# New cost figures for the block inverse in an emission planner, and smaller buffer demands in one scan

## The chip, the cores and the metric

The kernel runs on one core of a Trainium2 chip. The metric is the device time of one execution in microseconds. The profile is one execution, taken by the hardware profiler. Its engines are TensorE (PE for matmuls, PEld for weight loads), VectorE (DVE), ScalarE (ACT), GpSimd (POOL) and SyncE (SP), which issues all the DMAs.

## The reference, cut to what matters

Two layers run over 512 tokens of a main stream (x, width 1024) and 256 tokens of a context stream (c). In each layer one input projection feeds three head groups: a short gated convolution, a gated DeltaNet in both directions (4 heads of 128), and a spatial-gating MLP. An output projection and a SwiGLU feed-forward layer follow. In the last layer the context gives only the two final DeltaNet states.

```python
m = eye + where(strict, kkt * dmat * bc[..., None], 0)      # one triangular system per chunk, head and direction
sol = triangular_solve(m, rhs, lower=True, unit_diagonal=True)
u, w = sol[..., :dv], sol[..., dv:]
def _delta_update(s, w_c, u_c, kt_c, gl_c):
    v_new = u_c - w_c @ s
    return v_new, s * exp(gl_c) + kt_c.T @ v_new
```

The kernel solves these systems by inverting them, with chunks of 128 tokens, and then scans over the chunks with the state.

## The kernel before, in words

**A planner writes the program.** Each piece of the model is a Python generator (a task). While the program is built, a planner keeps one planned clock for each engine (`clk`: t for TensorE, v for VectorE, a for ScalarE, p for GpSimd, s and d for SyncE and the DMAs). Each helper (`vtt`, `vtrans`, `act`, `matmul`, `dma`) emits one instruction and calls `spend`, which adds a written cost, in us, to its engine's clock, after the operands' planned times. A task yields either a planned time, from which it may go on, or a condition. `run_tasks` always resumes the task with the lowest priority number of those that can go on at TensorE's planned time. The order in which the helpers are called is the order of the instructions on each engine, for SP's DMAs too. The costs are in no instruction: they only decide the order, which of two engines a copy goes to (`lighter`), and which buffer is taken.

**Buffers.** There are 66 small slots (128 x 512) and 13 large ones (128 x 1024). `room=n` in `gtile` lets a task go on only while n small slots are free. `stash` spills a finished tile to DRAM when its planned time comes, and `unstash` reads it back.

**Weights.** A `Feed` loads a weight tile (`wf`), rounds it to a high part (`wh`, on ACT or DVE) and subtracts to get a low part (`wl`, on DVE). The dense products read both parts.

**The block inverse** runs four times, once for each stream and layer: context of layer 0 (here c0), main of layer 0 (x0), context of layer 1 (c1), main of layer 1 (x1). `block_inverse` gathers the 32 x 32 diagonal blocks of eight matrices (four heads, two directions) into one tile, `iva`: for four of them by copies, for four by small transposes on DVE. One large transpose follows, then 31 row steps of two DVE instructions each (`ivt` = product, `ivv` = difference), each step followed by `yield self.pace()`, which waits until TensorE's planned clock is within 2 us of DVE's. Two large transposes write `iva` and `ivb`. Then four tasks (`substitute`) build `td` and `U` for two matrices each: GpSimd clears the tile, eight block copies fill `td` and `U` (64 for an inverse), matmuls form the product Q and join the blocks, and U is the inverse. `gdn_scan` waits for U. For context of layer 1 it runs with `kv_only`: it updates the states and gives no output.

```python
def vtt(self, out, a, b, op):
    self.nc.vector.tensor_tensor(out=out, in0=a, in1=b, op=op)
    self.spend("v", 0.07 + 1.04 * self.size(out), [out], [a, b])   # size: thousands of elements per partition
```

Tile names in the trace are those with which a slot was first named, so that a tile of one role may stand under another name.

Of the kernel before, what the change touches and what calls it, by code (L numbers as in the profile page):

```python
# [8 lines left out]
AF = mybir.ActivationFunctionType  # L9
ALU = mybir.AluOpType  # L10
AX = mybir.AxisListType

P = 128
# [269 lines left out]
class Builder:  # L283
# [221 lines left out]
        self.nc.vector.scalar_tensor_tensor(out=out, in0=in0, scalar=scalar, in1=in1, op0=op0, op1=op1)  # L505
        self.spend("v", 0.13 + 1.04 * self.size(out), [out], [in0, in1])

    def vtt(self, out, a, b, op):
        self.nc.vector.tensor_tensor(out=out, in0=a, in1=b, op=op)  # L509
        self.spend("v", 0.07 + 1.04 * self.size(out), [out], [a, b])  # L510

    def vts(self, out, a, s1, s2, op0, **kw):
        self.nc.vector.tensor_scalar(out, a, s1, s2, op0=op0, **kw)
# [9 lines left out]

    def vtrans(self, out, in_):
        self.nc.vector.transpose(out, in_)  # L525
        self.spend("v", 0.07 + 1.04 * self.size(out), [out], [in_])

    def ptt(self, out, a, b, op):
        self.nc.gpsimd.tensor_tensor(out=out, in0=a, in1=b, op=op)
# [2 lines left out]
    def round(self, out, in_):  # L532

        n = self.size(out)
        (self.act if self.lighter(v=0.07 + 0.52 * n, a=0.09 + 0.83 * n) == "a" else self.vcopy)(out, in_)

    def copy(self, out, in_):

        n = self.size(out)
        if in_.space == bass.MemoryType.PSUM:  # L540
            e = self.lighter(v=0.07 + 1.04 * n, a=0.05 + 0.83 * n)
        else:
            e = self.lighter(v=0.07 + 0.52 * n, a=0.09 + 0.83 * n)
        {"v": self.vcopy, "a": self.act}[e](out, in_)
# [784 lines left out]
    def block_inverse(self, st, G):  # L1329

        n, T = st.n, st.T
        yield lambda: "inverse" not in self.ev
        self.ev.add("inverse")
        self.wanted = 4
        yield lambda: self.lroom() >= 0
        self.wanted = 0
        bufs = [self.blk(s, 1024) for s in ("iva", "ivb", "ivv", "ivt")]
        C, X, V = (b.ap.rearrange("p (a b) -> p a b", b=32) for b in bufs[:3])
        tmp = bufs[3].ap
        if 8 * n < 32:  # L1340
            self.pset(C[:, 8 * n:, :], 0.0)
        for j in (0, 4, 1, 5, 2, 6, 3, 7):
            lt3 = G["Lt"][j].ap.rearrange("p (t c) -> p t c", c=P)
            for q in range(4):
                r = slice(32 * q, 32 * q + 32)
                blkd = lt3[r, :, r]
                dst = C[r, n * j:n * j + n, :]
                if j < 4:
                    self.copy(dst, blkd)
                else:  # L1350
                    self.vtrans(dst, blkd)
                self.pset(blkd, 0.0)
            yield self.pace()
        self.vtrans(X, C.rearrange("p s f -> p f s"))
        vf = bufs[2].ap
        self.pset(vf, 0.0)
        self.pset(vf[:, 0:1024:33], 1.0)
        for j in range(31):
            a, b = j + 1, 31 - j
            tm = tmp[:, :a * b].rearrange("p (i k) -> p i k", k=b)  # L1360
            xj = X[:, a:, j:j + 1].rearrange("p k o -> p o k")
            self.vtt(tm, V[:, 0:a, j:j + 1].to_broadcast([P, a, b]), xj.to_broadcast([P, a, b]), ALU.mult)
            self.vtt(V[:, 0:a, a:], V[:, 0:a, a:], tm, ALU.subtract)
            yield self.pace()

        E1, E2 = C, X
        self.vtrans(E1.rearrange("p s i -> p i s"), V)
        self.vtrans(E2.rearrange("p s k -> p k s"), V.rearrange("p i k -> p k i"))
        bufs[2].free()
        bufs[3].free()  # L1370
        sl = lambda t: slice(P * t, P * t + P)

        def substitute(js):
            yield self.room(4)
            td = self.blk("td", T)
            self.pset(td.ap, 0.0)
            v3 = lambda ap: ap.rearrange("p (t c) -> p t c", c=P)
            for j in js:
                lt, fwd = G["Lt"][j], j < 4
                us, ts = (E2, E1) if fwd else (E1, E2)  # L1380
                yield self.room(3)
                U = self.blk("U", T)
                self.pset(U.ap, 0.0)
                for q in range(4):
                    r = slice(32 * q, 32 * q + 32)
                    self.copy(v3(td.ap)[r, :, r], ts[r, n * j:n * j + n, :])
                    self.copy(v3(U.ap)[r, :, r], us[r, n * j:n * j + n, :])
                pq = yield from self.gtile(td.ap, lt.ap, room=2)
                for t in range(n):
                    self.matmul(pq[:, sl(t)], lt.ap[:, sl(t)], td.ap[:, sl(t)])  # L1390
                lt.free()
                Q = self.blk("Q", T)
                self.act(Q.ap, pq[:, :T], AF.Copy, scale=-1.0)

                for rows, cols in ((((0, 96), (32, 128)), ((0, 64), (64, 128)), ((0, 32), (96, 128))) if fwd else
                                   (((0, 128), (0, 96)), ((64, 128), (0, 64)), ((64, 128), (0, 32)))):
                    r, c = slice(*rows), slice(*cols)
                    pv = yield from self.gtile(Q.ap, U.ap)
                    for t in range(n):
                        self.matmul(v3(pv)[r, t, c], v3(Q.ap)[:, t, r], v3(U.ap)[:, t, c])  # L1400
                    if c.stop - c.start == 96:
                        self.vtt(v3(U.ap)[r, :, c], v3(pv)[r, :n, c], v3(U.ap)[r, :, c], ALU.add)
                    else:
                        r = slice(96, 128) if cols == (0, 32) else r
                        self.copy(v3(U.ap)[r, :, c], v3(pv)[r, :n, c])
                Q.free()
                G["U"][j] = U
            td.free()

        for i in range(self.NSUB):  # L1410
            self.spawn(K["psub"], substitute(range(i, 8, self.NSUB)))
        yield lambda: len(G["U"]) == 8
        bufs[0].free()
        bufs[1].free()
        self.ev.discard("inverse")
        G["inverse"] = True
# [25 lines left out]
    def gdn_scan(self, st, G, states, kv_only, keep_last):  # L1442

        n = st.n
# [4 lines left out]
        v3 = lambda ap: ap.rearrange("p (h c) -> p h c", c=P)  # L1449
# [3 lines left out]
        def direction(d):  # L1453
            for i in range(n):
# [2 lines left out]
                col = lambda key, h: G[key][:, t, 4 * d + h:4 * d + h + 1]  # L1457
                s, last = states[d], i == n - 1 and not keep_last
                if s is not None:
                    ps = yield from self.gtile(s, room=5)  # L1460
                    for h in hs:
                        self.matmul(ps[:, cs[h]], G["kT"][h].ap[:, c], s[:, cs[h]])
                    r = self.blk("r")
                    for h in hs:
                        self.stt(r.ap[:, cs[h]], ps[:, cs[h]], col("ego", h), vn[h].ap[:, c], ALU.mult, ALU.add)
                pv = yield from self.gtile(*([r.ap] if s is not None else []), room=4)
                for h in hs:
                    b = r.ap[:, cs[h]] if s is not None else vn[h].ap[:, c]
                    self.matmul(pv[:, cs[h]], G["U"][4 * d + h].ap[:, c], b)
# [48 lines left out]
        for d in K["dirs"]:  # L1518
            self.spawn(0, direction(d))
# [647 lines left out]
```

## Time and profile before

| | us |
|---|---|
| median of 3 runs | 1806.54 (1805.84 to 1809.01) |
| the profiled execution: its time | 1808.4 |
| the profiled execution: its span, first to last instruction | 1806.7 |
| PE busy / PEld busy | 1736.9 / 1488.1 |
| DVE busy / ACT busy / POOL busy | 1319.5 / 777.8 / 103.6 |
| mean granted TensorE clock | 0.985 of full speed |

The 1.7 us between time and span lie before the first and after the last instruction. Busy times are sums over the span, and the engines overlap: what an idle gap costs is read from the stretch in which it lies.

### The profile page before, as it was taken

The numbers are of one execution on the slowest core, as the hardware profiler recorded it, in microseconds if no ns is written. First come the engines' busy times: TensorE is split into PE (matmuls) and PEld (weight loads), VectorE is DVE, ScalarE is ACT, GpSimd is POOL, SyncE is SP. The second block draws the span as 40 slices with busy tenths as digits, with TensorE's granted clock in tenths as the row PEclk, the third lists the DMA queues.
The fourth block names the chain that finished last, engine by engine and source line by source line (L and its number), as shares of the span: only waits on it lengthen the run. The fifth ranks groups of instructions, "written<-read, shape, count | busy, mean of one in ns | idle before, by whom it ended". The sixth has DMA issues, their size and how long they took to land.

```text
span 1806.7 us, 27473 instructions
## 1 busy us (share of the span) xinstructions
PE 1736.9 (96%) x10271; PEld 1488.1 (82%) x10271; DVE 1319.5 (73%) x2510; ACT 777.8 (43%) x1685; POOL 103.6 (6%) x268
## 2 busy tenths in 40 slices
PE   6999999979999999999999999999899999999998
PEld 2588888869799888888788898888789798888886
DVE  1689869957769977633688866679968897667746
ACT  3764446253564232111364346467443754322222
POOL 0001002000000000000002000002000000000000
PEclk8899999989999999999999999999999999999999
DMA  8742212235578755533352435532334683234234
GB/s 285 251 141 84 83 40 71 85 105 171 158 222 269 227 183 187 161 111 113 96 167 84 126 107 167 164 92 79 107 96 136 197 231 101 90 109 128 82 94 139
DMA packets 288869, 250.14 MB, mean 138 GB/s; under 512 B 14544, under 2 KB 219350, under 8 KB 288736
## 3 DMA queue, kind: packets, MB, share of 16 engines
q1 hardware_dynamic: 288736, 248.40, 45.2%
q8 instruction: 80, 1.31, 0.3%
q14 instruction: 53, 0.43, 0.1%
HBM read 233.28 MB, written 15.07 MB: 137 GB/s over the span
## 4 chain that ended last, share of the span: by engine, by line
PE 34%; DVE 9%; ACT 3%; DMA 3%; issue 1%; POOL 1%; DVEq 0%; SPq 0%; POOLq 0%; ACTq 0%
PE ps L496 33%; DVE wl_l L509 2%; DMA wf_l<-in_w_in_dram 1%; DVE ivt_l L509 1%; DMA wf_l<-in_w_ffn_in_dram 1%; DVE ivv_l L509 1%; ACT wh_l L553 1%; DVE x_b L505 1%; DVE dt_b L509 1%; DVE acc_b L509 1%; PE ps L501 1%; DVE iva_l L525 0%; DVE ivb_l L525 0%; ACT xn_b L553 0%; ACT junk L553 0%
## 5 line engine op out<-in xcount | busy, mean ns | idle before, releaser
L496 PE MATMUL ps<-hh_b,wh_l 128*128 128x256 f32 (+2 forms) x2640 | 724.0, 324 | 7.6 <-DVE hh_b L505 3.3
L496 PE MATMUL ps<-hh_b,wl_l 128*128 128x512 f32 (+1 forms) x1960 | 655.2, 334 | 1.9 <-DVE wl_l L509 1.9
L496 PEld LDWEIGHTS ps<-hh_b,wh_l 128*128 128x128 f32 (+1 forms) x2640 | 458.5, 190 | 53.7 <-DVE hh_b L505 4.6
L496 PE MATMUL ps<-hl_b,wh_l 128*128 128x512 f32 (+3 forms) x1360 | 484.7, 357 | 0.0
L509 DVE TENSOR_TENSOR wl_l<-wf_l,wh_l 128x1024 fp32r<-128x1024 f32 (+1 forms) x310 | 375.7, 1214 | 145.2 <-ACT wh_l L553 115.8
L496 PEld LDWEIGHTS ps<-hh_b,wl_l 128*128 128x128 f32 x1960 | 374.1, 191 | 40.6 <-DVE wl_l L509 2.8
L553 ACT ACTIVATE wh_l<-wf_l 128x1024 fp32r<-128x1024 f32 (+2 forms) x218 | 226.9, 1043 | 324.7 <-PE ps L496 117.5
L496 PEld LDWEIGHTS ps<-hl_b,wh_l 128*128 128x128 f32 (+1 forms) x1360 | 257.7, 190 | 37.3 <-issue 1.7
L496 PE MATMUL ps<-wh_l,ah_b 128*128 128x512 f32 x576 | 201.6, 390 | 0.0
L496 PE MATMUL ps<-wl_l,ah_b 128*128 128x512 f32 x424 | 165.3, 390 | 1.1 <-DVE wl_l L509 1.1
L505 DVE SCALAR_TENSOR_TENSOR macc_b<-mw_b,csilu,macc_b 128x512 f32<-128x512 f32 x182 | 132.6, 747 | 16.2 <-DMA mw_b<-in_w_mod_dram 9.7
L496 PEld LDWEIGHTS ps<-wh_l,ah_b 128*128 128x128 f32 x576 | 108.1, 188 | 22.5 <-issue 0.3
L517 DVE CAST wh_l<-wf_l 128x1024 fp32r<-128x1024 f32 (+1 forms) x95 | 64.9, 684 | 69.2 <-PE ps L496 46.1
L496 PE MATMUL ps<-wh_l,al_b 128*128 128x512 f32 x272 | 105.9, 389 | 0.0
L496 PEld LDWEIGHTS ps<-wl_l,ah_b 128*128 128x128 f32 x424 | 79.6, 188 | 18.0 <-DVE wl_l L509 1.9
L553 ACT ACTIVATE ah_b<-at_b 128x512 fp32r<-128x512 f32 (+1 forms) x76 | 40.6, 538 | 121.4 <-DVE at_b L509 121.4
L553 ACT ACTIVATE at_b<-ps 128x512 f32<-128x512 f32 (+1 forms) x70 | 33.6, 481 | 119.6 <-PE ps L496 114.4
L496 PE MATMUL ps<-wh_l,yh_b 128*128 128x512 f32 x192 | 73.8, 402 | 0.1
L509 DVE TENSOR_TENSOR at_b<-ps,at_b 128x512 f32<-128x512 f32 (+1 forms) x70 | 38.4, 549 | 43.7 <-PE ps L496 43.7
L496 PE MATMUL ps<-wl_l,yh_b 128*128 128x512 f32 x160 | 62.8, 393 | 0.0
L509 DVE TENSOR_TENSOR ivt_l<-ivv_l,ivb_l 128x31 f32<-128x31 f32 (+15 forms) x124 | 60.0, 484 | 3.4
L509 DVE TENSOR_TENSOR acc_b<-ps,acc_b 128x512 f32<-128x512 f32 x92 | 59.6, 683 | 3.0 <-PE ps L496 3.0
(528 smaller groups left out, 2183.8 us busy)
## 6 DMA issues: line engine op xcount, KB each, us to landing
wf_l<-in_w_ffn_in_dram SPq DMA_DIRECT2D x132, 512.0 KB
mw_b<-in_w_mod_dram SPq DMA_DIRECT2D x208, 256.0 KB
wf_l<-in_w_ffn_out_dram SPq DMA_DIRECT2D x66, 512.0 KB
wf_l<-in_w_in_dram SPq DMA_DIRECT2D x64, 512.0 KB
wf_l<-in_w_o_dram SPq DMA_DIRECT2D x32, 512.0 KB
us_b<-sd SPq DMA_DIRECT2D x26, 256.0 KB
xd<-x_b SPq DMA_DIRECT2D x20, 256.0 KB
x_b<-xd SPq DMA_DIRECT2D x20, 256.0 KB
```

The lines of the kernel that those rows point to most:

```text
L496: self.nc.tensor.matmul(out, lhsT, rhs, start=start, stop=stop, skip_group_check=more)
L501: self.nc.tensor.transpose(out, in_, self.ident[:m, :m])
L505: self.nc.vector.scalar_tensor_tensor(out=out, in0=in0, scalar=scalar, in1=in1, op0=op0, op1=op1)
L509: self.nc.vector.tensor_tensor(out=out, in0=a, in1=b, op=op)
L517: self.nc.vector.tensor_copy(out, in_)
L553: self.nc.scalar.activation(out=out, in_=in_, func=func, **kw)
```

## The change

The costs of the block inverse's own DVE and ACT instructions are replaced in the planner, and a state-only scan asks for 3 and 2 free small slots where it asked for 5 and 4. No instruction's operands are changed.

```diff
-    def vtt(self, out, a, b, op):
+    def vtt(self, out, a, b, op, fixed=0.07, each=1.04):
         self.nc.vector.tensor_tensor(out=out, in0=a, in1=b, op=op)
-        self.spend("v", 0.07 + 1.04 * self.size(out), [out], [a, b])
+        self.spend("v", fixed + each * self.size(out), [out], [a, b])
...
     def vtrans(self, out, in_):
         self.nc.vector.transpose(out, in_)
-        self.spend("v", 0.07 + 1.04 * self.size(out), [out], [in_])
+        self.spend("v", 0.13 + 1.85 * self.size(out), [out], [in_])
...
+    def copy_block(self, out, in_):
+
+        n = self.size(out)
+        if self.lighter(v=0.16 + 0.55 * n, a=0.21 + 0.85 * n) == "a":
+            self.nc.scalar.activation(out=out, in_=in_, func=AF.Copy)
+            self.spend("a", 0.21 + 0.85 * n, [out], [in_])
+        else:
+            self.nc.vector.tensor_copy(out, in_)
+            self.spend("v", 0.16 + 0.55 * n, [out], [in_])
...
                 if j < 4:
-                    self.copy(dst, blkd)
+                    self.copy_block(dst, blkd)
                 else:
                     self.vtrans(dst, blkd)
...
-            self.vtt(tm, V[:, 0:a, j:j + 1].to_broadcast([P, a, b]), xj.to_broadcast([P, a, b]), ALU.mult)
-            self.vtt(V[:, 0:a, a:], V[:, 0:a, a:], tm, ALU.subtract)
+            self.vtt(tm, V[:, 0:a, j:j + 1].to_broadcast([P, a, b]), xj.to_broadcast([P, a, b]), ALU.mult, 0.17, 1.92)
+            self.vtt(V[:, 0:a, a:], V[:, 0:a, a:], tm, ALU.subtract, 0.2)
...
-                    self.copy(v3(td.ap)[r, :, r], ts[r, n * j:n * j + n, :])
-                    self.copy(v3(U.ap)[r, :, r], us[r, n * j:n * j + n, :])
+                    self.copy_block(v3(td.ap)[r, :, r], ts[r, n * j:n * j + n, :])
+                    self.copy_block(v3(U.ap)[r, :, r], us[r, n * j:n * j + n, :])
...
-                    ps = yield from self.gtile(s, room=5)
+                    ps = yield from self.gtile(s, room=3 if kv_only else 5)
...
-                pv = yield from self.gtile(*([r.ap] if s is not None else []), room=4)
+                pv = yield from self.gtile(*([r.ap] if s is not None else []), room=2 if kv_only else 4)
```

The copy that `copy_block` replaces was planned at 0.07 + 0.52 n on DVE and 0.09 + 0.83 n on ACT.

## Rows read from the trace of the kernel before

**Rows 1.** The page's busy time: us, share of the span, instructions.

```profile
PE 1736.9 (96%) x10271; PEld 1488.1 (82%) x10271; DVE 1319.5 (73%) x2510; ACT 777.8 (43%) x1685; POOL 103.6 (6%) x268
```

**Rows 2.** Windows of 20 us: PE, PEld, DVE, ACT, POOL busy, PEclk, DMA share, GB/s.

```profile
180.00:200.00 20.00, 17.28 (x86) 13.72 (x85) 19.35 (x40) 6.57 (x10) 2.17 (x8) 0.91 0.28 79
...
360.00:380.00 20.00, 8.69 (x65) 8.31 (x64) 13.62 (x41) 13.12 (x35) 3.67 (x7) 0.74 0.38 122
...
440.00:460.00 20.00, 16.62 (x93) 13.89 (x92) 14.90 (x31) 11.86 (x41) 5.00 (x5) 1.00 0.73 240
...
1020.00:1040.00 20.00, 16.84 (x112) 15.89 (x111) 15.16 (x27) 12.75 (x31) 0.32 (x1) 0.83 0.68 185
...
1300.00:1320.00 20.00, 14.26 (x74) 11.34 (x73) 18.05 (x46) 10.07 (x27) 1.57 (x2) 0.83 0.10 27
...
1740.00:1760.00 20.00, 20.00 (x90) 16.57 (x89) 8.35 (x10) 3.98 (x5) 0.00 (x0) 1.00 0.32 105
```

**Rows 3.** One window of 4 us behind the gap of x0.

```profile
376.00:380.00 4.00, 4.00 (x26) 3.89 (x27) 2.86 (x11) 2.24 (x7) 0.00 (x0) 0.53 0.00 0
```

**Rows 4.** Groups and tiles, block inverse: busy and mean ns, or ns min/median/max.

```profile
L509 DVE TENSOR_TENSOR ivt_l<-ivv_l,ivb_l 128x31 f32<-128x31 f32 (+15 forms) x124 | 60.0, 484 | 3.4
L509 DVE TENSOR_TENSOR ivv_l<-ivv_l,ivt_l 128x31 f32<-128x31 f32 (+15 forms) x124 | 42.4, 342 | 3.7
L525 DVE STREAM_TRANSPOSE ivb_l<-iva_l 128x1024 f32<-128x1024 f32 x4 | 8.4, 2092 | 0.4
L525 DVE STREAM_TRANSPOSE iva_l<-lt_b 32x128 f32<-32x128 f32 x32 | 9.6, 301 | 0.8
L517 DVE COPY U_b<-iva_l 32x128 f32<-32x128 f32 x18 | 3.9, 219 | 0.2
L553 ACT ACTIVATE td_b<-iva_l x30: 252/305/313, 209.7 to 1306.9; 32x128 f32<-32x128 f32 x18, 32x64 f32<-32x64 f32 x12
```

**Rows 5.** ACT's timeline where x0, c1 and x1 end: start, us, idle before.

```profile
357.93 0.63 ACT L553 ACTIVATE td_b<-iva_l 32x128 f32<-32x128 f32 x2 [10.14 <-issue]
358.58 0.39 ACT L553 ACTIVATE z_b<-ps 128x256 f32<-128x256 f32 x1
...
1021.56 2.12 ACT L553 ACTIVATE U_b<-iva_l 32x64 f32<-32x64 f32 x8 [13.01 <-DVE iva_l L525]
1023.71 1.06 ACT L553 ACTIVATE wh_l<-wf_l 128x1024 fp32r<-128x1024 f32 x1
...
1299.24 0.96 ACT L553 ACTIVATE td_b<-iva_l 32x128 f32<-32x128 f32 x3 [10.04 <-DVE iva_l L525]
...
1300.59 1.15 ACT L553 ACTIVATE vt_b<-ps 128x256 f32<-128x256 f32 x4
```

**Rows 6.** PE's timeline at the four inverses.

```profile
194.47 0.44 PE L501 MATMUL ps<-ident,vn_b 128*128 128x128 f32 x2 [2.72 <-ACT vn_b L553]
...
360.89 2.02 PE L496 MATMUL ps<-td_b,lt_b 128*128 128x128 f32 x16
...
375.83 6.26 PE L496 MATMUL ps<-U_b,Q_b 128*96 128x96 f32 x64 [11.31 <-ACT Q_b L553]
...
1024.82 0.58 PE L496 MATMUL ps<-hh_b,wh_l 128*128 128x256 f32 x1 [2.00 <-ACT wh_l L553]
...
1308.15 1.12 PE L496 MATMUL ps<-wst,vt_b 128*64 128x128 f32 x8 [4.97 <-ACT ac_b L553]
```

**Rows 7.** SP and ACT in the timeline of x0's gap.

```profile
365.36 0.39 SPq L472 DMA_DIRECT2D wf_l<-in_w_o_dram  x1
...
369.48 1.06 ACT L553 ACTIVATE wh_l<-wf_l 128x1024 fp32r<-128x1024 f32 x1 [4.31 <-DMA wf_l<-in_w_o_dram]
```

**Rows 8.** DVE and POOL in the same stretch.

```profile
363.36 2.31 DVE L517 COPY U_b<-ivb_l 32x128 f32<-32x128 f32 x2
...
363.88 1.45 POOL L547 MEMSET U_b<- 128x512 f32 x3
```

**Rows 9.** DVE's timeline at the state-only scan's first product.

```profile
1065.55 0.69 DVE L509 TENSOR_TENSOR v_b<-ps,bt_c 128x512 f32<-128x512 f32 x1 [0.81 <-PE ps L496]
```

## The prediction, made before the changed kernel was run

> **What bounds the kernel now.** I read the page's busy times first [rows 1]. PE is busy for 1736.9 of 1806.7 us, so only 69.8 us of the span are open to an edit that changes nothing but order, plus what a slow clock costs. The Trainium skill speaks against this reading (Perfetto Trace Analysis, Identifying the Most-Contended Engine): matmul busy time does not tell how near TensorE is to its limit, and the share of weight loads is to be used. By that rule up to 1806.7 - 1488.1 = 318.6 us would be open. The trace does not bear that out here: in a stretch late in the feed-forward layer where PE has no gap and a full clock, PEld is busy for 16.57 of 20 us, 83% [rows 2]. The page's 82% is thus what back-to-back products look like in this kernel, and I keep the 69.8.
>
> Next I looked for the gaps, with windows of 20 us. Each of the four inverses has one near its end [rows 2]: 20 less PE's busy time is 2.72 at c0, 11.31 at x0, 3.16 at c1 and 5.74 at x1, together 22.9 us. Behind each the granted clock is lower for a while (half speed is the lower of its two levels, 1.2 GHz). One less the clock, times 20, bounds the cost: 1.8 at c0, 3.4 at c1, 3.4 at x1. At x0 most of the slow time lies in the gap itself, so I take the stretch after it, 4 busy us at 0.53: 0.47 x 4 = 1.9 [rows 3]. That makes 10.5. What the change can give back at the inverses is therefore at most 22.9 + 10.5 = 33.4 us, 1.8%.
>
> Then I asked the timelines what holds PE in each gap. **In ACT's queue the block copies stand too early.** Before the first copy out of the transposed tile ACT sits idle for 10.14 us at x0, 13.01 at c1 and 10.04 at x1, and the instruction right behind is something that PE or DVE wants [rows 5]: at x0 a gate tile (z_b), at c1 the rounding of a weight (wh_l), at x1 the token-major copy (vt_b). PE then waits 2.00 for that wh_l at c1, and 4.97 at x1 for the normalised vt [rows 6]; there the row names another tile of ACT, but what the product reads is vt. At x0 the chain is longer: late z_b copies hold back spills on SP, the next output-projection weight is issued only at 365.36, ACT waits 4.31 for it with its rounding, and Q's copy stands behind that [rows 7], so that PE loses 11.31 [rows 6]. At c0 PE waits 2.72 for an ACT step on a value tile [rows 6]; I put that down to DVE's queue before it, which is busy for 19.35 of 20 us there [rows 2].
>
> So the planner thought the inverse done about 10 to 13 us before it was.
>
> **The change part by part.** Per inverse, the written costs before and after, and what the rows say [rows 4]:
> - Row steps: the products and differences cover the sum of (j+1)(31-j), 5456 elements. Before: 62 x 0.07 + 2.08 x 5.456 = 15.7 us. After: 31 x 0.37 + 2.96 x 5.456 = 27.6. Measured: (60.0 + 42.4) / 4 = 25.6. The planner gains 11.9.
> - Three large transposes: 1.13 before and 2.02 after, measured 2.09: 2.7 more.
> - Sixteen small transposes, 32 x 128: 0.20 before, 0.37 after, measured 0.30: 2.6 more.
> - Eighty block copies of that size: DVE 0.14 to 0.23, measured 0.22; ACT 0.20 to 0.32, measured 0.305. About 0.11 each, 8.6 over two engines. The ratio of the two engines' costs hardly moves (0.70 to 0.72), so the split between them should stay.
>
> The first three make 17.2 us on DVE before the copies can start, against a measured ACT wait of 10 to 13. The new costs thus cover the lag that I see, and overshoot it somewhat.
>
> Nothing of this is executed: no instruction becomes faster or goes away. What moves: row steps are spread over more of TensorE's planned time, since each waits until DVE's planned clock is within 2 us; other DVE work (wl, value tiles, normalisation) goes between them; block copies go behind roundings and gate copies in ACT's queue; and with them the spills and loads in SP's queue and the clears of td and U in POOL's. Cost of the moved instructions themselves: nothing, since their DVE and ACT time is the same; DVE's load in these windows (19.35 of 20 at c0 [rows 2]) is the cover that is thin, and without it a late wl costs PE its full lateness.
>
> What I count as given back, between nothing and 33.4:
> - c1: all of 3.2 + 3.4 = 6.6. A wh_l simply stands behind a copy that should come later.
> - x1: two thirds of 5.7 + 3.4, 6.1. The copies of vt can go first, but normalisation still shares DVE with the last transposes.
> - x0: half of 11.3 + 1.9, 6.6. The first part of its chain is ACT's early wait, the second is a weight that arrives late.
> - c0: half of 2.7 + 1.8, 2.3, as the order on DVE is only partly mended.
>
> Sum 21.6. Against it: work that goes ahead of the row steps makes the inverse end later, and behind each x inverse the scan has then less dense work beside it. At x0 PE begins with td at 360.89, only 3 us after the first copy, so nothing is spare there [rows 5, 6]. Some 80 us later PE already has a gap of 20 - 16.62 = 3.4 [rows 2]; I take that once more for each of x0 and x1, and 2.7, the smallest gap above, for a new order elsewhere: 9.5. The bounds of this term are 0 and 17.2 a place.
>
> **The looser room in the state-only scan: nothing.** Its first product's DVE step at 1065.55 waited 0.81 for PE, not for a buffer [rows 9], and the states it gives are read only by the scan behind x1, whose copies start at 1299.24 [rows 5], over 230 us later. Without that cover it could cost or give a microsecond. It may matter as a permission where the new order leaves fewer free slots.
>
> **A price the planner still leaves out.** Two block copies on DVE took 2.31 us instead of 0.44 while POOL cleared tiles [rows 8, 4]. The Trainium skill (SBUF — State Buffer, Who interferes with whom) says that such a DVE copy and a GpSimd instruction exclude each other for their whole length. By the row this costs 1.9 us in one place, and DVE idles afterwards. As a mechanism of this kernel: twelve clears an inverse, 1.45 / 3 = 0.48 us each on x, could hold a copy each time: 5.8 at each x inverse and half that at each c inverse, 17 in all.
>
> **Sum.** 1808.4 - 21.6 + 9.5 = 1796.3 for a profiled execution. The profiled one stands 1.9 above the median of the runs shown, so the median should be 1794.5.
>
> **The rivals.** About 0.2%, 3.6 us, is what a measurement of this kernel can tell from no change: faster means under 1802.9, slower over 1810.1.
> - *Part of the stalls go, some come back* (my forecast): 1794.5, own range 1784 to 1802.5. Chance 0.54.
> - *All of it comes back and nothing is lost*: 1806.5 - 33.4 = 1773, or down to 1784 with a loss. For it: the same sign at x0, c1 and x1 [rows 5]. Against: at x0 the late weight [rows 7]. Chance 0.11.
> - *The stall only moves*: ACT no longer stands before the copies, but PE waits instead for Q and U, as the inverse's chain on DVE is no shorter, and DVE is full. 1803 to 1810. The change then does nothing for the time. Chance 0.12.
> - *Slower: at x0 the dense work runs out.* If the copies leave up to 17.2 us later and no gate or projection product is left for PE, its gap grows from 11.3 by as much. The other places give 15.0 - 9.5 = 5.5; so this decides once x0's gap grows by over 9.1 us, to more than 20.4. At its full price: 1806.5 - 5.5 + 17.2 = 1818. For it: no slack at x0. Against: DVE's work is the same, and the lag of 10 us already happens. Chance 0.20.
> - *Slower by the port rule*: more copies fall beside clears, 17 us on DVE, of which PE would have to see over 16. 1811. Only one pair of copies shows it. Chance 0.03.
>
> **How the numbers follow.** Faster: 0.54 + 0.11 = 0.65. Same: 0.12. Slower: 0.20 + 0.03 = 0.23. The predicted time is the first case's. The range runs from 1779, which leaves out half of the second case, to 1814, which leaves out about half of the fourth: some 0.15 in all.
>
> **What would show it.** In the changed profile the ACT waits before the first copy out of iva should fall from 10 to 13 us to under 4, the row steps should be further apart with wl between them, and the clock behind each inverse should stay near 1. Instruction counts and mean durations should be the same to within a few copies that changed engine. Wrong would be: ACT waits as long as before (the planner's lag had another cause), the gap at x0 over 20 us, or a new gap of several us between 440 and 480 or after x1's scan. If the inverse windows mend and the total does not, the loss stands outside them, in the order of the feed-forward layers.

## The result, and the profile after

| | before | after |
|---|---|---|
| median of 6 runs, us | 1807.22 (1805.55 to 1810.94) | 1826.01 (1825.20 to 1831.35) |
| ratio after / before | | 1.0095, 95% interval 1.008 to 1.011 |
| the profiled execution / its span | 1808.4 / 1806.7 | 1825.2 / 1823.5 |
| mean granted TensorE clock | 0.985 | 0.983 |

The kernel became 0.95% slower, some 17 us by the ratio. The prediction was 1794.5 us with a range up to 1814.

The first view is the page's busy time (as [rows 1]).

```profile
PE 1743.0 (96%) x10271; PEld 1489.0 (82%) x10271; DVE 1315.0 (72%) x2490; ACT 784.0 (43%) x1711; POOL 100.2 (5%) x268
```

The counts of PE and POOL are the same; DVE has 20 instructions fewer and ACT 26 more, so more than a few copies chose the other engine. The span is 16.8 us longer: PE is idle for 80.5 us instead of 69.8, and busy for 6.1 us more with the same number of instructions. The Trainium skill (Perfetto Trace Analysis, Identifying the Most-Contended Engine) says that TensorE's headroom is to be judged by MFU (the matmul rate over the peak) and by the busy time of its weight loads, and not by that of its matmuls. The trace agrees in so far that PEld grew by 0.9 us only, so the 6.1 us are the same work taking longer and not more work.

Next, windows of 20 us (as [rows 2]; columns PE, PEld, DVE, ACT, POOL busy, PEclk, DMA share, GB/s).

```profile
360.00:380.00 20.00, 15.62 (x70) 12.03 (x69) 19.04 (x46) 8.07 (x14) 0.00 (x0) 0.83 0.54 179
380.00:400.00 20.00, 15.47 (x67) 11.67 (x66) 16.79 (x20) 10.51 (x22) 2.13 (x4) 0.99 0.80 240
400.00:420.00 20.00, 12.49 (x77) 11.66 (x78) 16.41 (x37) 16.41 (x39) 6.04 (x10) 0.66 0.43 141
420.00:440.00 20.00, 17.76 (x182) 17.14 (x180) 12.48 (x25) 16.36 (x38) 1.05 (x2) 1.00 0.58 163
440.00:460.00 20.00, 18.76 (x154) 17.79 (x155) 10.19 (x16) 5.85 (x14) 0.00 (x0) 0.83 0.38 116
...
1040.00:1060.00 20.00, 17.19 (x139) 16.87 (x140) 14.46 (x26) 12.78 (x26) 0.00 (x0) 1.00 0.69 189
...
1180.00:1200.00 20.00, 16.29 (x114) 15.65 (x115) 12.12 (x23) 13.75 (x30) 0.70 (x1) 0.83 0.39 111
...
1320.00:1340.00 20.00, 17.85 (x100) 14.15 (x99) 16.14 (x39) 8.35 (x18) 2.10 (x3) 1.00 0.46 124
```

The one gap of 11.31 at x0 is gone; five windows in a row with smaller gaps stand in its place, three of them with a slow clock. I add up, over all windows of a stretch, PE's idle time and (1 - PEclk) x 20. The second term also counts a slow clock while PE is idle, which costs nothing, so it is a bound:

| stretch, us | before | after |
|---|---|---|
| 180 to 360 | 2.8 + 1.8 = 4.6 | 2.6 + 1.8 = 4.4 |
| 360 to 540 | 16.5 + 5.2 = 21.7 | 22.4 + 13.8 = 36.2 |
| 540 to 980 | 2.4 + 0.0 = 2.4 | 4.9 + 0.0 = 4.9 |
| 980 to 1240 | 9.7 + 5.2 = 14.9 | 12.6 + 3.4 = 16.0 |
| 1240 to 1480 | 10.7 + 3.4 = 14.1 | 10.7 + 0.0 = 10.7 |

So x0 and what follows it lose 14.5 us by these sums, more of it (8.6) in clock than in idle time (5.9). The layer-1 inverses together are a little better.

What PE waits for (us in all, times, the longest): the wait for the normalised stream (tile xn_b) has doubled from 12.8 us, and ACT's Q, the 11.3 of [rows 6], is gone.

```profile
PE ps L501 <- ACT xn_b L563: 24.1, 9, 8.6
PE ps L496 <- DMA mw_b<-in_w_mod_dram: 6.7, 3, 4.6
PE ps L496 <- DVE wl_l L509: 5.7, 8, 1.6
```

The timelines around x0's end, DVE, POOL, ACT and PE (start, us, idle before). The first line is of the kernel before, the others are of the changed one:

```profile
357.70 2.15 DVE L525 STREAM_TRANSPOSE ivb_l<-ivv_l 128x1024 f32<-128x1024 f32 x1
...
379.07 2.04 DVE L525 STREAM_TRANSPOSE iva_l<-ivv_l 128x1024 f32<-128x1024 f32 x1
382.07 2.17 DVE L525 STREAM_TRANSPOSE ivb_l<-ivv_l 128x1024 f32<-128x1024 f32 x1
...
390.45 0.53 POOL L557 MEMSET td_b<- 128x512 f32 x1 [31.35 <-DVE macc_b L505]
...
391.01 0.95 ACT L541 ACTIVATE td_b<-iva_l 32x128 f32<-32x128 f32 x3 [1.02 <-POOL td_b L557]
...
407.39 2.58 PE L501 MATMUL ps<-ident,xn_b 128*128 128x128 f32 x10 [8.58 <-ACT xn_b L563]
...
423.52 1.06 PE L496 MATMUL ps<-td_b,lt_b 128*128 128x128 f32 x8
```

The transposed tiles are there at 384, but the first substitution product runs at 423.52, 39 us later; in the kernel before they were there at 359.85 and it followed 1 us later ([rows 6]: 360.89). Between them PE works off the context's output projection until 396, then waits 1.68 us for a load and 8.58 us for the context's normalisation, a chain over ACT, DVE, GpSimd and PE, with nothing else to do, and from 409.68 on runs products of the context's feed-forward layer. GpSimd's clear of td waits as well, for a slot that another task's accumulator still holds.

At c1 and x1, ACT in front of the copies and PE behind them (as [rows 5] and [rows 6]):

```profile
1038.74 2.12 ACT L541 ACTIVATE td_b<-iva_l 32x64 f32<-32x64 f32 x8 [12.98 <-DVE iva_l L525]
1040.89 1.06 ACT L563 ACTIVATE wh_l<-wf_l 128x1024 fp32r<-128x1024 f32 x1
...
1042.00 0.39 PE L496 MATMUL ps<-hh_b,wh_l 128*128 128x256 f32 x1 [2.01 <-ACT wh_l L563]
...
1314.71 1.91 ACT L541 ACTIVATE td_b<-iva_l 32x128 f32<-32x128 f32 x6 [9.06 <-DVE iva_l L525]
```

ACT waits 12.98 and 9.06 where it waited 13.01 and 10.04, and at c1 the same late wh_l costs PE the same 2.0 us.

**The build sorts again.** Last, the stretch of x0's row steps, before and after:

```profile
320.80:355.40 34.60, 34.60 (x199) 30.55 (x198) 32.88 (x73) 6.95 (x9) 2.63 (x5) 1.00 0.26 77
...
344.60:378.70 34.10, 29.72 (x153) 24.55 (x153) 32.28 (x76) 12.16 (x22) 0.74 (x2) 0.91 0.60 192
```

It is as long as before (34.1 us against 34.6), and of its 76 DVE instructions 61 are row steps. Yet in the planner's calls 45 other DVE instructions stand between the steps (5 in the kernel before). I had written that the order of the calls is the order on each engine. For DVE that is wrong: behind the planner, the build orders the instructions once more and draws the row steps together again. TensorE's order stays nearly as called: 3% of its instructions fall outside the longest run that keeps the order of the calls, against a third of DVE's and over a third of ACT's. So the longer plan moved only TensorE's side: counted in the planner's own TensorE costs, the work ahead of the first substitution product grew by 19.7 us at c0, 35.3 at x0, 24.2 at c1 and 4.0 at x1 (good to 0.1).

The sorting also made the ACT rows that the prediction rests on. In the kernel before already, the z_b, wh_l and vt_b that ACT runs right behind its first block copies [rows 5] had been called ahead of all of them. At x0, c1 and x1, 3, 8 and 10 ACT instructions were called ahead of the inverse's first block copy on ACT and stand behind it in the built program; with the new costs they are 32, 26 and 13. So the planner had not put the copies too early: the build drew them forward, and did so again with the new costs.

### The profile page after: what moved, and what is told of

The parts are those of the page before. It is cut to its first block, busy times and chain, and to the rows that moved or that the text cites. A ratio compares the mean times of both kernels' runs of the same rounds, so it can differ in the third digit from the quotient of the medians.

```text
span 1823.5 us, 27451 instructions
## 1 busy us (share of the span) xinstructions
PE 1743.0 (96%) x10271; PEld 1489.0 (82%) x10271; DVE 1315.0 (72%) x2490; ACT 784.0 (43%) x1711; POOL 100.2 (5%) x268
## 5 line engine op out<-in xcount | busy, mean ns | idle before, releaser
L505 DVE SCALAR_TENSOR_TENSOR macc_b<-mw_b,csilu,macc_b 128x512 f32<-128x512 f32 x182 | 132.1, 746 | 13.8 <-DMA mw_b<-in_w_mod_dram 7.7
L496 PEld LDWEIGHTS ps<-wh_l,ah_b 128*128 128x128 f32 x576 | 108.2, 188 | 22.4 <-issue 0.3
```

What stands on the lines that cost most here:

```text
L496: self.nc.tensor.matmul(out, lhsT, rhs, start=start, stop=stop, skip_group_check=more)
```

## The experiments

Theory: TensorE's new order at x0 makes the loss, as the context's normalisation now stands ahead of the substitution that used to cover it. Rivals: each inverse loses its own few us; the extra TensorE work, or buffers that come free late, cost time by themselves; any other order costs something, and the order before was a lucky one.

All 18 runs in one table. "Ahead" is the planned TensorE work ahead of x0's first product, over that of the kernel before. "Lag" is how much later PE has done its 4000th of 10271 instructions (660 us in the kernel before), interpolated from the 20 us windows of one profile each. It is good to some 4 us: e2's TensorE order up to there is that of the kernel before.

| run | edit | ratio to before (95%) | ahead | lag |
|---|---|---|---|---|
| after | | 1.0095 (1.0080 to 1.0110) | +35.3 | +17.8 |
| e1 | new costs in layer 0 only | 1.0091 (1.0076 to 1.0106) | +35.3 | +19.5 |
| e2 | new costs in layer 1 only | 1.0043 (1.0031 to 1.0056) | 0 | +4.3 |
| e3 | new costs at x0 only | 1.0005 (0.9991 to 1.0020) | +23.3 | -3.4 |
| e4 | new costs but at x0 | 1.0025 (1.0015 to 1.0035) | +23.2 | +5.6 |
| e5 | after, normalisation held | 1.0029 (1.0018 to 1.0040) | +23.3 | +7.2 |
| e6 | before, x0's substitution late | 1.0032 (1.0022 to 1.0043) | +26.8 | +7.1 |
| e7 | new costs at x0 and x1 | 1.0024 (1.0009 to 1.0039) | +23.3 | +4.3 |
| e8 | after, row steps 10 us ahead | 1.0094 (1.0078 to 1.0111) | +12.7 | +15.8 |
| e9 | after, early clears | 1.0128 (1.0109 to 1.0148) | +35.3 | +21.0 |
| e10 | before, latency 0.14 | 1.0106 (1.0086 to 1.0125) | +8.1 | +17.8 |
| e11 | before, transpose 0.04 | 0.9998 (0.9986 to 1.0009) | +5.5 | +3.2 |
| e12 | as e5, c1 with old costs | 1.0039 (1.0026 to 1.0052) | +23.3 | +7.4 |
| e13 | after, 2.2 ahead | 1.0096 (1.0078 to 1.0114) | +23.7 | +21.2 |
| e14 | after, transpose 0.04 | 1.0096 (1.0076 to 1.0115) | +46.5 | +19.5 |
| e15 | after, latency 0.14 | 1.0044 (1.0028 to 1.0059) | +67.8 | +6.4 |
| e16 | before, latency 0.12 | 1.0045 (1.0029 to 1.0062) | +0.2 | +5.6 |
| e17 | before, 2.2 ahead | 1.0039 (1.0024 to 1.0053) | 0 | +2.6 |
| e18 | after, latency 0.12 | 1.0099 (1.0082 to 1.0116) | +78.3 | +23.3 |

**Where: costs switched inverse by inverse (e1 to e4, e7).** In each, the cost of steps, transposes and copies is chosen by a table over c0, x0, c1, x1; the looser room stays.

```diff
+STEPS, TRANS, COPIES = (1, 1, 0, 0), (1, 1, 0, 0), (1, 1, 0, 0)
+    # this is e1; e2 has (0, 0, 1, 1), e3 (0, 1, 0, 0), e4 (1, 0, 1, 1), e7 (0, 1, 0, 1), three times each
...
+        mul = ((0.07, 1.04), (0.17, 1.92))[STEPS[i]]      # i counts the inverses
...
-            self.vtt(tm, ..., ALU.mult, 0.17, 1.92)
+            self.vtt(tm, ..., ALU.mult, *mul)
```

> New costs only at the two inverses of layer 0 (c0 and x0); c1 and x1 keep the old ones; looser room kept. Theory (the loss is made at x0: 35 us of TensorE's planned work more stand ahead of x0's first substitution product, while DVE finishes the row steps as early as before): about as slow as the changed kernel, 14 to 20 us over the kernel before. Rival (each of the four inverses loses its own few us): about half, 7 to 11 over. Second rival (any new order costs something by chance): no place in particular, anything from 0 to 20 over, and the same for the next three.

> New costs only at the two inverses of layer 1 (c1 and x1). Theory: the order up to c1 is that of the kernel before, so nothing of the loss at x0 is there, and what c1 and x1 give back (about 3 us of slow clock at each, little of the gaps) shows: 0 to 7 us under the kernel before. Rival (every inverse loses): 7 to 11 over.

> New costs at x0 alone. The built program has 23 us of TensorE's planned work more ahead of x0's first product instead of 35. Theory: two thirds of the loss, 8 to 14 us over the kernel before. Rival (every inverse loses its own): 3 to 6 over.

> Old costs at x0, new ones at the other three. Since c0 now ends later in the plan, 23 us more TensorE work still stand ahead of x0's first product, although x0's own costs are the old ones. Theory (it is the work ahead of the product that counts, not whose costs are written): 5 to 12 us over the kernel before. Rival (the costs written at x0 make the loss): 0 to 5 under, as in the run with layer 1 alone.

> New costs at the two inverses of the main stream, old ones at the context's. At x0 21 us of the context's output projection go ahead of the product and the normalisation stays behind it, as in the run with x0 alone. Theory (layer 1 loses through c1, which uses up the work that covers the main stream's own normalisation near 1165; x1 gains back about 3): 0 to 6 us under the kernel before. Rival (x1's new costs lose too): 2 to 8 over.

e1 is the theory's: the whole loss is made in layer 0, and its stretch 360 to 540 has 36.9 us of idle time and slow clock, as after has 36.2. The others are mixed. e3 loses nothing, with 23.3 us more work ahead of x0's product (a miss for both sides): there only the output projection went ahead, the normalisation stayed behind the product, and the stretch has 16.1 us. So work ahead is no loss by itself. e4 is 5 us slower, at the edge of its range, but not by the mechanism given: its stretch 360 to 540 has 19.9 us, less than before, so that number is luck. e2 was to gain and loses 0.43%; there PE waits, behind c1's scan, for the main stream's normalisation, with the clock at 0.85 in the window 1160 to 1180, and after has that gap too, at 1183:

```profile
1176.54 1.97 PE L502 MATMUL ps<-ident,xn_b 128*128 128x128 f32 x8 [5.06 <-ACT xn_b L564]
```

The pieces don't add up, 0.91% and 0.43% against 0.95%. e7 misses and lands on its rival, 4 us over: x1's new costs gave nothing.

**The cause at x0: hold the normalisation (e5), or put it ahead under old costs (e6).**

```diff
+self.ev.add(f"product_{st.name}")            # e5: in substitute, behind the first product
 ...
 yield from self.post_norm(sc, cx, rc[0])
 hc.clear()
+yield on("product_x")                        # e5: ahead of the context's pre-norm
 ...
+if st.name == "x":                           # e6, in the kernel before: ahead of the four substitute tasks
+    yield lambda: "hc_ffn" in self.ev
+    yield self.clk["t"] + 12.0
```

> The changed kernel, with one line added: the context's normalisation after its output projection waits until x0's first substitution product has been emitted, so that product, joins and scan of x0 stand in TensorE's queue behind the projection (21 us of planned work) but ahead of the feed-forward layer that needs the normalised context. All new costs stay. Theory (the loss at x0 is that the normalisation, a chain over ACT, DVE and PE, has lost the substitution as its cover): between 360 and 540 the gaps and the slow clock shrink from 36 to about 20 us, and the time falls by 10 to 15 us, to some 1811 to 1816. Rival (the extra TensorE work ahead of the product makes the loss by itself, or buffers that come free late): 21 to 23 us still stand ahead, so half of the loss or more remains, 1817 to 1822.

> The kernel before, all costs old and no looser room, with two lines added: x0's substitution is emitted only after the context's normalisation and 12 us of planned time. Theory: the order alone makes the loss, 8 to 16 us over the kernel before, with the waits for the normalised context (xn_b) that the changed kernel shows. Rival (the costs or the looser room matter in another way than through this order): within 4 us of the kernel before.

e5 takes the ratio from 1.0095 to 1.0029, which is 0.66% or 12 us back, with all new costs in place. Windows and PE's timeline of e5:

```profile
400.00:420.00 20.00, 15.75 (x128) 14.22 (x129) 16.34 (x32) 15.27 (x41) 5.03 (x7) 0.83 0.62 201
420.00:440.00 20.00, 19.91 (x200) 18.17 (x197) 15.47 (x39) 12.81 (x28) 0.52 (x1) 1.00 0.44 126
440.00:460.00 20.00, 20.00 (x181) 19.94 (x180) 17.93 (x51) 4.03 (x7) 0.00 (x0) 1.00 0.16 47
```

```profile
398.13 0.83 PE L496 MATMUL ps<-td_b,lt_b 128*128 128x128 f32 x6
...
410.53 1.97 PE L501 MATMUL ps<-ident,xn_b 128*128 128x128 f32 x8 [0.63 <-ACT xn_b L563]
```

The products now stand ahead of the normalised tile, whose wait fell from 8.58 to 0.63 us; the stretch 360 to 540 has 20.4 us, as expected. The total alone would not show the cause, since unrelated changes of order move it as much (e10 below); the wait and the stretch do. e6, the test the other way round, makes that wait without any new cost, but loses only 0.32% (6 us), between the 8 to 16 us expected and the rival's 4: the wait has taken the place of the 11.31 us gap, and 360 to 540 comes to 20.6 us as before; what it loses shows behind, 8.7 us from 540 to 980 where the kernel before has 2.4. PE's timeline of e6:

```profile
396.25 1.97 PE L501 MATMUL ps<-ident,xn_b 128*128 128x128 f32 x8 [10.60 <-ACT xn_b L553]
```

**The buffers (e9).**

```diff
 self.vtt(V[:, 0:a, a:], V[:, 0:a, a:], tm, ALU.subtract, 0.2)      # in the row steps
+if st.name == "x" and len(early) < 8 and self.slots.room() >= 9:
+    early.append(self.blk("td" if len(early) % 2 == 0 else "U", T))
+    self.pset(early[-1].ap, 0.0)
 ...                                         # and substitute takes these tiles first
```

> The changed kernel, but at the main stream's inverses (x0, x1) td and U of four matrices take their slots and are cleared during the row steps, so that the block copies need not wait for a slot that the context's normalisation still holds (in the changed kernel GpSimd's clear of td at 390.45 had waited 31 us for it). TensorE's order is that of the changed kernel, with 35 us more ahead of x0's product. Theory (TensorE's order is the cause; the product stands behind the normalisation anyway): the clears and copies at x0 go some 10 to 20 us earlier and the time stays, 1821 to 1829. Rival (the slots that come free late are the cause): 8 to 15 us faster than the changed kernel, 1811 to 1818.

```profile
354.72 0.53 POOL L557 MEMSET td_b<- 128x512 f32 x1 [9.31 <-PE ps L496]
...
379.87 1.90 ACT L541 ACTIVATE td_b<-iva_l 32x128 f32<-32x128 f32 x6 [3.22 <-DVE iva_l L525]
...
411.36 2.58 PE L501 MATMUL ps<-ident,xn_b 128*128 128x128 f32 x10 [9.31 <-ACT xn_b L563]
...
426.95 1.06 PE L496 MATMUL ps<-td_b,lt_b 128*128 128x128 f32 x8
```

The clears and the first copies come early, the copies by 11 us, and the first product still stands behind the normalisation. The buffer rival falls. The run is slower than expected, too: 1832.9 us, with 39.0 us in the stretch 360 to 540, which I have not explained.

**Row steps kept together in the plan (e8), and c1 back to old costs (e12).**

```diff
-            yield self.pace()
+            yield self.pace(ahead=10.0)      # e8, in the row steps
+STEPS, TRANS, COPIES = (1, 1, 0, 1), (1, 1, 0, 1), (1, 1, 0, 1)      # e12, with the two lines of e5
```

> The changed kernel with row steps that may run 10 us ahead of TensorE's planned clock instead of 2, so that fewer other instructions are emitted between them, as the built program has it anyway. 13 us more TensorE work than in the kernel before stand ahead of x0's product, 14 at c0, 2 less at c1, 4 more at x1. Theory (the loss comes of a plan that stretches the row steps over 47 to 61 us where the built program runs them in 34 to 40): most of the loss goes, 1803 to 1813. Rival (true costs lose whatever the stretch): 1818 to 1828.

> The kernel that holds the context's normalisation behind x0's first product, with c1's costs back to the old ones: 29 us less TensorE work ahead of c1's product than with the new ones. Theory (c1's longer plan uses up the work that covers the main stream's normalisation near 1165, a gap of 5 us with 3 us of slow clock in the runs with new costs at c1): 4 to 8 us faster than with c1 new, 1806 to 1811 where the held kernel has some 1815. Rival (what is left above the kernel before is chance of order): the same as the held kernel or worse, 1813 to 1820.

Both theories miss, and both runs land where their rivals stood (1826.4 and 1816.3). In e8 PE waits, between 355 and 480, 8.1 us for the context's gated output (yh_b, from ACT) and 4.5 for the scan's output: an order with less work ahead loses as much, by other waits of the same chain. In e12 the gap near 1180 is gone (980 to 1240: 11.5 us), but 1240 to 1480 has 17.9 instead of e5's 11.5.

**Chance: one small figure changed, under old and under new costs (e10, e11, e13 to e18).**

```diff
-LAT = dict(t=0.2, v=0.13, ...)
+LAT = dict(t=0.2, v=0.14, ...)               # e10 (before), e15 (after); 0.12: e16 (before), e18 (after)
-self.spend("t", 0.109 if m == P else 0.03, [out], [in_])
+self.spend("t", 0.109 if m == P else 0.04, [out], [in_])     # e11 (before), e14 (after)
-K = {'ahead': 2.0,
+K = {'ahead': 2.2,                           # e17 (before), e13 (after)
```

> The kernel before with one planner figure changed by a hundredth of a microsecond that has nothing to do with the inverse (the latency after a DVE instruction, 0.13 to 0.14). It gives another order almost from the start: 8 us more TensorE work ahead of x0's product. Theory (a named order at x0 and at c1 makes the differences): within 4 us of the kernel before. Rival (the order before was a lucky one, and any other costs something): 4 to 10 us over, as in the runs with layer 1 alone, all but x0, or x0 and x1.

> As the one before, with another figure: the cost of a small TensorE transpose, 0.03 to 0.04. 5.5 us more TensorE work ahead of x0's product. Theory: within 4 us of the kernel before. Rival (any other order costs something): 4 to 10 us over. If the two small changes land on both sides, or far apart, the size of what an order does by chance is seen.

> The changed kernel, and tasks may run 2.2 us ahead in the plan instead of 2.0. In the built order 24 us more TensorE work than in the kernel before stand ahead of x0's first product; the context's output projection is in them, its normalisation stands behind the product. Theory (the place of the normalisation at x0 decides): as the held kernel, 0 to 9 us over the kernel before. Rival (true costs lose as such): 15 to 22 over. Chance alone names no value.

> The changed kernel, with 0.04 instead of 0.03 for a small TensorE transpose. 46 us more TensorE work ahead of x0's first product, the context's normalisation 23 us ahead of it. Theory: 14 to 26 us over the kernel before, with the wait for the normalised context again near 400. Chance alone: anything from 0 to 20.

> The changed kernel, with 0.14 instead of 0.13 for the latency after a DVE instruction. 68 us more TensorE work ahead of x0's first product: the context's normalisation stands 44 us ahead, and its whole gated half of the feed-forward layer goes before the product too. Theory: 14 to 30 us over, since the normalisation has no cover and the scan of x0, later still, has less dense work beside it. Chance alone: anything from 0 to 20.

> The kernel before with 0.12 instead of 0.13 for the latency after a DVE instruction. The work ahead of x0's first product is that of the kernel before (0.2 us more), and the context's output projection stands between and behind the products. Theory: within 4 us of the kernel before. Chance alone: as likely 5 to 20 over as not.

> The kernel before, and tasks may run 2.2 us ahead in the plan instead of 2.0: the partner with old costs of the run with the new ones and 2.2. The order at x0 is that of the kernel before; from c1 on it differs. If true costs lose as such, the old partner lies near the kernel before (0 to 5 over); if any order but the tuned one loses, 5 to 19 over. From the order alone (nothing is changed up to c1) I expect 0 to 5.

> The changed kernel with 0.12 instead of 0.13 for the latency after a DVE instruction: the partner with new costs of the run with the old ones and 0.12, which lay 8 us over. 78 us more TensorE work ahead of x0's product. If true costs lose as such: 12 to 25 over the kernel before, above its partner. If they don't: as likely below its partner's 8 as above.

In e10 a figure moved by a hundredth of a microsecond, with no bearing on the inverse, makes the kernel before 1.06% slower: as much as the whole change. Two windows of e10:

```profile
360.00:380.00 20.00, 9.21 (x39) 7.44 (x38) 18.17 (x45) 11.59 (x33) 1.94 (x4) 0.66 0.36 114
...
460.00:480.00 20.00, 9.34 (x43) 6.78 (x42) 15.75 (x27) 12.98 (x33) 6.59 (x3) 0.69 0.78 259
```

It keeps x0's old gap (PE waits 10.8 us for z_b) and gets 10.66 us of idle time in a second window, in the context's chain again (xn_b 5.3, yh_b 3.4). e11 (0 us over) and e14 (17 over, with a wait of 9.2 us for the normalised context) landed where the theory put them. e16 and e17, both some 8 us over, did not, and e18 (20 over) is where it was expected if true costs lose as such. Nor did e13 and e15: e13 has the normalisation behind the product and loses 0.96%, as its rival had it, waiting for other links of that chain, as its waits between 340 and 660 show:

```profile
PE ps L496 <- DVE macc_b L505: 5.2, 1, 5.2
PE ps L496 <- DVE yh_b L509: 4.7, 2, 4.4
PE ps L501 <- ACT modr_b L563: 4.3, 1, 4.3
```

e15 has the normalisation 44 us ahead, waits 8.8 us for it, and loses only 0.44%. So the place of the normalisation explains the step from after to e5, and is no rule for other orders.

Old against new costs in five pairs, ratio less 1 in per cent: 0 and 0.95 (unchanged figures), 1.06 and 0.44, -0.02 and 0.96, 0.39 and 0.96, 0.45 and 0.99. The mean difference is 0.48, with a 95% interval of -0.3 to 1.3 (standard deviation 0.65, five pairs). That the new costs lose on the whole is likely from these, not shown.

What the runs agree on is the place: the eight programs with a loss of 0.9% or more, after among them, all lag by 15.8 us or more at 660 us, the eleven others by at most 7.4. Idle time and slow clock between 360 and 980 us, summed as above, separate the same programs: 41.1 to 47.8 us in the eight, 20.0 to 30.7 in the eleven, 24.1 in the kernel before.

## Why the prediction was wrong

- *"So the planner thought the inverse done about 10 to 13 us before it was"*: this step failed first, and the change was built on it. ACT's waits are in the rows; that the planner's costs made them I had read off the order in the trace. The calls show otherwise: z_b, wh_l and vt_b were called ahead of the copies, and the build put them behind. The prediction named the sign, "ACT waits as long as before (the planner's lag had another cause)", and it came: 12.98 us for 13.01 at c1, 9.06 for 10.04 at x1.
- *Row steps spread, with wl and other work between them* ("What moves"): this failed for the same reason. It holds in the plan and not in the built program, where the steps stay together and only TensorE gets more work ahead. Shown by the stretch of row steps and by the counts of helper calls.
- *"The new costs thus cover the lag that I see"*: failed with them. ACT's waits should have fallen under 4 us. Only x0's 10.14 went, where the whole inverse came 24 us later, among other work.
- *Given back, 21.6.* c1: 6.6 forecast; the window behind it lost its slow clock (3.4) and kept its gap, and the gap near 1183 cost 3.7 and 3.4 of clock. x1: 6.1 forecast, 3.4 came (14.1 to 10.7). c0: 2.3 forecast, 0.2 came. x0: 6.6 forecast; the 11.31 gap went, but nothing is left of it in the stretch.
- *Lost, 9.5.* Mis-sized. I took 3.4 for x0, a gap that the profile before already showed; the stretch came out 14.5 worse on balance. I looked behind the scan for dense work that runs out, and not ahead of the substitution for a serial chain that would lose its cover. That chain did not bind in the kernel before, so its row was small.
- *The rivals.* The outcome is on the side of "slower: at x0 the dense work runs out" (0.20). Its mechanism is not what happened: no gap at x0 is over 8.58 us, and the copies left late with PE busy elsewhere. The port rule was not needed. The range ended at 1814.
- *The looser room, nothing*: right as costed. With the old costs it gives the same instruction order on every engine, so it can move no time. It matters as the permission that I named: with the new costs and the old demands the plan comes to a point where no task can go on, so the costs alone give no program.
- *A step that wasn't in the prediction*: how far the time hangs on the order as such. Four unrelated nudges under old costs gave 0 to 1.06%, up to 19 us: about the 21.6 that I expected back, and twice the 9.5 of loss. As far as these four show, a forecast from the change's meaning that came closer than that would have been luck.

Open: whether true costs are worse on the whole; which of the three cost groups (steps, transposes, copies) does most, as they weren't run apart; what makes the 0.29% that is left in e5; and by what the build sorts. No version beat the kernel before: e3 and e11 equal it.

## What to carry to other kernels

Where a planner writes the order, look first at what the built program does with it, engine by engine, before an order seen in a trace is put down to the planner: here one engine followed the plan and another did not, and truer costs for the second moved only the first. Ask of every piece of dense work that is drawn forward which serial chain it was covering. And before a change of order is judged by its total, nudge an unrelated figure a few times: here that alone moved the time by up to 1%.

## What was not expected of the hardware

The slow clock can account for more of x0's loss than idle time. Within 360 to 540 the granted clock is at its lower level (half speed, 1.2 GHz) in one spell before and in three after. The spells' ends are read from windows of half a microsecond; the first line is of the kernel before:

```profile
369.50:379.50 10.00, 3.67 (x23) 3.67 (x24) 8.09 (x28) 8.55 (x23) 0.00 (x0) 0.50 0.33 117
...
372.50:379.50 7.00, 6.28 (x15) 3.99 (x14) 6.63 (x21) 4.46 (x7) 0.00 (x0) 0.51 0.23 78
400.00:413.50 13.50, 6.11 (x27) 5.50 (x28) 12.17 (x25) 10.39 (x22) 5.05 (x8) 0.50 0.63 209
441.00:447.50 6.50, 6.26 (x34) 6.20 (x35) 2.86 (x5) 1.40 (x5) 0.00 (x0) 0.50 0.36 107
```

Before, the clock fell inside the gap of 11.31 us, and PE was busy for only 3.67 of the 10 slow us. After, three spells behind shorter gaps have 18.65 busy us at half speed. Half of the difference, 7.5 us, bounds what the clock adds; the idle time grew by 5.9. So here several gaps of 2 to 9 us left more work at a slow clock than one of 11, most of whose slow spell fell on idle time.
